# First stage of a two-layer backbone: token stores in pieces, third buffers, and scratch tiles that share room

## Chip, cores and metric

The kernel runs on one core of one Trainium2 chip. The metric is the device time of one execution in microseconds; before the change it is 5293.11 us, the median of three runs (5286.99 to 5300.15).

## What is computed

One inference step of a hybrid backbone with two layers. A layer normalises and modulates the tokens (256 context tokens and 2048 latent ones), projects them, runs four mixers on the projections, and maps their gated outputs back into the residual:

```python
h = (rms_norm(x) * (1.0 + scale) + shift).astype(dt)
(da_q, da_k, da_v, da_g, s5_u, s5_g, hg_q, hg_ff, hg_fb, hg_i, hg_g,
 mla_cq, mla_ckv, mla_kr, mla_g) = split_columns(h @ P["w_in"][l])
a_out, a_ctx = diff_attn_branch(...)
b_out, b_ctx = s5_branch(...)
c_out, c_ctx = hgrn_branch(...)
d_out, d_ctx = mla_branch(...)
mixed = jnp.concatenate([a_out, b_out, c_out, d_out], axis=-1)
x = (x.astype(F32) + gate * (mixed @ P["w_out"][l]).astype(F32)).astype(dt)
```

The change touches the projection of the keys, queries and values (`da_q`, `da_k`, `da_v`, part of the MLA inputs) and the tables that the state-space branch `s5_branch` needs: powers of the discretised diagonal transition matrix, its products with the input and output matrices, and the skip term `s5_d`.

## The kernel before

A layer has three parts: `first_stage`, `mixers`, `out_proj`. `first_stage` weaves two generators, `proj1` and `s5_build`; a scheduler decides with a simulated timeline in which order each engine gets their instructions, and each engine then runs its own list strictly in order. The order of PE in the mixers is written by hand. All stores and loads named below are issued by SP, one list too, so a store whose data are late holds up whatever stands behind it; only the value stores `VT` of the last block are issued by POOL.

**proj1** (L420) works on six blocks of 384 tokens. `h_block` (L275) normalises a block: PE transposes (`pst`, L299), ACT scales (`t32`, L304), DVE casts to the high part `hhi` (L171) and subtracts to the low part `hlo` (L173), for eight slices `kc` of 128 channels. `keep(i)` (L438) then stores both parts of the block to `HD` (L440), from where proj2 reads all tokens again. Five products `psF` follow (two of keys, two of queries, one of the MLA inputs; 24 matmuls each), each with `evac1` (L358): ACT copies (`x`), DVE rotates (`sh`, `rt`), ACT casts `sphi` and DVE subtracts `splo`, and three stores take them to `KD` or `QD` (L355). The MLA rows use the same tiles under the names `krhi` and `krlo`. Then come three value products `psT` (24 matmuls each); ACT copies each to `evT` (L499), which is stored to `VT` (L500). `sphi`, `splo` and `evT` have two buffers each.

**s5_build** (L1160) makes tables for 16 channel groups. `prep(gi)` runs on POOL (`wz`, `so`, with the one scratch tile `tw`) and DVE (`so` at L1286, `cp`, `brep`); `emit(gi)` has PE transpose `wz` (`pswz`, L1302) and multiply (`psk`, L1307), ACT copy both, and SP store `so` to `SC`. After every fourth `emit` DVE adds the skip term `Db` to four finished tables `mp` (L1311); the last such addition belongs to group 15. POOL then doubles a small table `b` four times (`double_table`, L1150) with the scratch tile `t3`, and from it makes eight pairs of tables `Eb`, 28 operations per pair, each stored by two `ED` stores (L1336). `Eb0`, `Eb1` and `Db` have room of their own, and `t3` is free once the discretisation is done, so the scheduler is free to put `Eb` work between the `prep` steps:

```python
    emit(15, *late)
    E.memset(b_[0][:, :, 0:1], 1.0)
    ...
    double_table(E, b_, ph, slice(0, 16), t3, 0, 4)
    ...
    for g0 in range(0, 16, 2):
        gs = slice(g0, g0 + 2)
        Eb = [pb.tile([128, 2, 257], F32, tag=f"Eb{i}", name=f"Eb{i}") for i in range(2)]
```

**mixers** begins with proj2 (L506), led by attention's first pass (`psS`, from `ks` and `qs`, which are loaded from `KD` and `QD`). proj2 loads the normalised tokens back (`h<-HD`, L521) and a weight block at a time (`w<-wF`, L532, one tile `w32`). ACT and DVE split the first two weight blocks into `whi` and `wlo`, POOL the later ones.

Of the kernel before, what the change touches and what calls it, by code (L numbers as in the profile page):

```python
# [10 lines left out]
F32 = mybir.dt.float32  # L11
F32R = mybir.dt.float32r
# [95 lines left out]

PR = (0, 0)
AVB = 2  # L110
PPB = 3
# [163 lines left out]
def h_block(g, l, tok0, n, p, hi, lo, mod):  # L275
    nc = g.nc
    xs, ds = [], []
    for t in range(n // 128):
        xt = p.tile([128, D], F32, tag="xt", name="xt", bufs=3)
        nc.sync.dma_start(xt, x_src(g, l, tok0 + t * 128))  # L280
        ss = p.tile([128, 1], F32, tag="ss", name="ss")
        junk = p.tile([128, D], BF16, tag="junk", name="junk", bufs=1)
        nc.scalar.activation(out=junk, in_=xt, func=AF.Square, accum_out=ss)
        r = p.tile([128, 1], F32, tag="r", name="r")
        rsqrt_col(g, p, r, ss, 1.0 / D, "rs")
        dg = p.tile([128, 128], F32, tag="dg", name="dg", bufs=4)
        nc.vector.tensor_scalar(dg, g.ident, r, None, ALU.mult)
        xs.append(xt)
        ds.append(dg)
    cut = min(max(LS - tok0, 0), n)  # L290
    if mod is not None:
        next(mod)
    for kc in range(8):
        if mod is not None and kc % 2 == 0:
            next(mod)
            next(mod)
        ps = pst(g, "mm", "pst")
        for t in range(n // 128):
            nc.tensor.matmul(ps[:, t * 128:(t + 1) * 128], lhsT=xs[t][:, kc * 128:(kc + 1) * 128], rhs=ds[t], start=True, stop=True)  # L299
        t32 = p.tile([128, 384], F32, tag="t32", name="t32")  # L300
        for a, b, gr in ((0, cut, 0), (cut, n, 1)):
            if b > a:
                sc, sh = g.scale[:, gr, kc:kc + 1], g.shift[:, gr, kc:kc + 1]
                nc.scalar.activation(out=t32[:, a:b], in_=ps[:, a:b], func=AF.Identity, bias=sh, scale=sc)  # L304
        split2(g, hi[:, kc, :], lo[:, kc, :], t32, "vec")
    if mod is not None:
        run(mod)
# [36 lines left out]
def store_kr(g, p, src, tok0, n):  # L344
    nc = g.nc
    hi = p.tile([128, 384], F32R, tag="sphi", name="krhi")[64:96, :n]
    lo = p.tile([128, 384], F32R, tag="splo", name="krlo")[64:96, :n]
    split2(g, hi, lo, src)
    nc.sync.dma_start(g.KRD[0, 0:32, tok0:tok0 + n], hi.bitcast(F32))
    nc.sync.dma_start(g.KRD[1, 0:32, tok0:tok0 + n], lo.bitcast(F32))  # L350
# [7 lines left out]
def evac1(g, l, p, kind, idx, ps, tok0, n):  # L358
    nc = g.nc
# [15 lines left out]
    r32 = rope(g, p, x32, (0, 128), tok0, n, "rp")  # L375
    hi = p.tile([128, 384], F32R, tag="sphi", name="sphi")
    lo = p.tile([128, 384], F32R, tag="splo", name="splo")
    split2(g, hi, lo, r32)
# [27 lines left out]
def cache_keys(g, l, p):  # L406
    nc = g.nc
    for i in range(2):
        kc32 = p.tile([128, 384], F32, tag="x32", name="kc32", bufs=1)
        nc.sync.dma_start(kc32[:, :256], g.A["cdk"][l, i])  # L410
        hi = p.tile([128, 384], F32R, tag="sphi", name="sphi")
        lo = p.tile([128, 384], F32R, tag="splo", name="splo")
        split2(g, hi[:, :256], lo[:, :256], kc32[:, :256])
        store_qk(g, g.KD, (0, 1, 0), i, hi[:, :256], lo[:, :256], slice(NT, NK))
# [5 lines left out]
def proj1(g, l):  # L420
    nc = g.nc
    N = 384
    with ExitStack() as es:
# [7 lines left out]
        def prep(i):  # L431
# [4 lines left out]
            hs[i] = (hi, lo)  # L436

        def keep(i):  # L438
            for part, x in enumerate(hs[i]):
                nc.sync.dma_start(g.HD[part, :, :, starts[i]:starts[i] + N], x.bitcast(F32))  # L440

# [24 lines left out]
        for kc in range(0, 8, 2):  # L466
            w32 = pws.tile([128, 2, 512], F32, tag="w32", name="wt32")
            nc.sync.dma_start(w32, g.A["wT"][l, :, kc:kc + 2, :])
            split2(g, wth[:, kc:kc + 2, :], wtl[:, kc:kc + 2, :], w32, "act", W1LO)
        keep(0)  # L470
        yield
        cache_keys(g, l, p)
        for i, tok0 in enumerate(starts):
            if 0 < i < len(starts) - 1:
                prep(i + 1)
                keep(i + 1)
            if i == 2 and l == 0:
# [4 lines left out]
            for k, (kind, idx, cols) in enumerate(FB1):  # L482
                if i == 0 and k == H1:
                    prep(1)
                    keep(1)
                m = len(cols)
# [5 lines left out]
            for t in range(N // 128):  # L492
# [3 lines left out]
                for kc in range(8):  # L496
                    mm3(nc, ps, hi[:, kc, ts_], lo[:, kc, ts_], wth[:, kc, :], wtl[:, kc, :], kc == 0, kc == 7)
                o = p.tile([128, 512], F32, tag="ev", name="evT")
                nc.scalar.copy(o, ps)  # L499
# [660 lines left out]
def s5_build(g, l, p1, pb):  # L1160
# [64 lines left out]
    yield 5  # L1225
    t3 = pb.tile([128, 16, 16], F32, name="t3")
    den, fr, fi, am1 = t16("den"), t16("fr"), t16("fi"), t16("am1")
# [26 lines left out]
    for i in range(2):  # L1254
# [7 lines left out]
        V.tensor_copy(pt[i][64:128, :, 0:8][:, :, ::-1], pv[64:128, :, 0:8])  # L1262
    Db = pb.tile([128, 16, 16], F32, name="Db")
    nc.sync.dma_start(Db.rearrange("p g h -> p (g h)"), g.A["s5_d"][l:l + 1, :].to_broadcast([128, 256]))
# [51 lines left out]
    for gi in range(16):  # L1316
# [4 lines left out]
        late = x  # L1321
    emit(15, *late)
    E.memset(b_[0][:, :, 0:1], 1.0)
    E.memset(b_[1][:, :, 0:1], 0.0)
    double_table(E, b_, ph, slice(0, 16), t3, 0, 4)
    yield 5
    for g0 in range(0, 16, 2):
        gs = slice(g0, g0 + 2)
        Eb = [pb.tile([128, 2, 257], F32, tag=f"Eb{i}", name=f"Eb{i}") for i in range(2)]
        te = t3.rearrange("p (a b) c -> p a (b c)", a=2)  # L1330
# [477 lines left out]
```

## Time and profile before

| | |
|---|---|
| median of three runs | 5293.11 us (5286.99 to 5300.15) |
| the profiled execution's own time | 5296.69 us |
| its span, first to last instruction | 5294.9 us |
| mean granted clock of TensorE | 0.935 |
| busy: PE, DVE, ACT, POOL | 89%, 72%, 60%, 21% |
| chain that ended last | PE 49%, DVE 18%, DMA 13%, ACT 10%, issue 4%, POOL 4% |
| DMA bytes | 599.37 MB |
| first stage, layer 0 | until the first weight load of proj2 at 453.75 us |
| first stage, layer 1 | until the first weight load of proj2 at 3098.75 us |

The shares are means over stages with different limits. The first stage takes about 450 us of each layer; the times below are microseconds from the start of the span, layer 1 begins at some 2640 us. "Idle before" in a row names what the engine waited for; a wait for several things is put down to the one that came last.

### The profile page before, as it was taken

The numbers are of one execution on the slowest core, as the hardware profiler recorded it, in microseconds if no ns is written. First come the engines' busy times: TensorE is split into PE (matmuls) and PEld (weight loads), VectorE is DVE, ScalarE is ACT, GpSimd is POOL, SyncE is SP. The second block draws the span as 40 slices with busy tenths as digits, with TensorE's granted clock in tenths as the row PEclk, the third lists the DMA queues.
The fourth block names the chain that finished last, engine by engine and source line by source line (L and its number), as shares of the span: only waits on it lengthen the run. The fifth ranks groups of instructions, "written<-read, shape, count | busy, mean of one in ns | idle before, by whom it ended". The sixth has DMA issues, their size and how long they took to land.

```text
span 5294.9 us, 81097 instructions
## 1 busy us (share of the span) xinstructions
PE 4724.9 (89%) x27920; PEld 3434.4 (65%) x27920; DVE 3835.7 (72%) x7616; ACT 3183.3 (60%) x7516; POOL 1089.4 (21%) x1323
## 2 busy tenths in 40 slices
PE   6787999999998997898987879999999989989899
PEld 5676767677665664445776757676776656654477
DVE  7655767676668886896676657676766688879877
ACT  3225878777777783235433258787777777743354
POOL 4651222222210000000227712222222100000022
PEclk8998999999998997899999989999999989989999
DMA  6555233433332124415445452334333321241253
GB/s 219 170 174 154 87 105 96 130 116 104 92 88 75 47 57 129 130 50 148 157 155 200 159 167 86 108 94 130 116 103 93 88 73 48 54 117 52 75 155 126
DMA packets 507523, 599.37 MB, mean 113 GB/s; under 512 B 147630, under 2 KB 414806, under 8 KB 507110
## 3 DMA queue, kind: packets, MB, share of 16 engines
q1 hardware_dynamic: 506630, 592.61, 37.3%
q8 instruction: 220, 3.60, 0.3%
q14 instruction: 193, 1.58, 0.1%
q0 software_dynamic: 480, 1.57, 0.1%
HBM read 378.42 MB, written 215.18 MB: 112 GB/s over the span
## 4 chain that ended last, share of the span: by engine, by line
PE 49%; DVE 18%; DMA 13%; ACT 10%; issue 4%; POOL 4%; SPq 1%; ACTq 0%; DVEq 0%; POOLq 0%
PE psav L858 5%; PE psS L870 4%; PE psF L177 4%; PE psF L178 4%; PE psF L179 4%; PE psS L817 4%; PE psmav L950 3%; ACT junk L820 3%; PE psM L961 2%; DVE nm L818 2%; DVE a L872 2%; DVE mnm L927 2%; ACT pp L871 2%; PE psM L926 2%; PE pshg L1018 2%
## 5 line engine op out<-in xcount | busy, mean ns | idle before, releaser
L818 DVE TENSOR_REDUCE nm<-psS 128x1 f32<-128x512 f32 (+1 forms) x1312 | 790.5, 626 | 351.7 <-PE psS L817 340.5
L820 ACT ACTIVATE junk<-psS,nm 128x512 bf16<-128x512 f32 (+1 forms) x1312 | 848.7, 647 | 202.2 <-DVE nm L818 182.4
L871 ACT ACTIVATE pp<-psS 128x512 f32<-128x512 f32 (+1 forms) x1184 | 654.5, 594 | 165.7 <-PE psS L870 159.6
L177 PE MATMUL psF<-h,whi 128*128 128x288 f32 x2304 | 697.9, 303 | 32.8 <-ACT whi L169 32.8
L872 DVE SCALAR_TENSOR_TENSOR a<-pp,nlam 128x512 f32<-128x512 f32 (+1 forms) x592 | 510.3, 864 | 257.6 <-ACT pp L871 256.9
L178 PE MATMUL psF<-h,whi 128*128 128x288 f32 x2304 | 687.9, 299 | 0.0
L179 PE MATMUL psF<-h,wlo 128*128 128x288 f32 x2304 | 685.1, 297 | 1.8 <-DVE wlo L173 1.8
L964 ACT ACTIVATE me<-psM 128x512 f32<-128x512 f32 (+1 forms) x592 | 345.6, 590 | 440.8 <-PE psM L963 395.1
L817 PE MATMUL psS<-ks,qs 96*128 96x512 f32 (+1 forms) x1312 | 544.5, 425 | 58.9 <-ACT junk L820 37.7
L870 PE MATMUL psS<-qs,ks 98*128 98x512 f32 (+1 forms) x1184 | 440.6, 436 | 53.9 <-ACT junk L820 38.7
L177 PEld LDWEIGHTS psF<-h,whi 128*128 128x128 f32 x2304 | 444.7, 193 | 65.3 <-ACT whi L169 34.5
L171 POOL CAST whi<-w 128x1024 fp32r<-128x1024 f32 x140 | 153.2, 1094 | 1622.0 <-PE psF L178 1299.7
L178 PEld LDWEIGHTS psF<-h,whi 128*128 128x128 f32 x2304 | 444.8, 193 | 54.8
L927 DVE TENSOR_REDUCE mnm<-psM 128x1 f32<-128x512 f32 (+1 forms) x656 | 394.1, 623 | 70.9 <-PE psM L926 69.0
L179 PEld LDWEIGHTS psF<-h,wlo 128*128 128x128 f32 x2304 | 441.5, 192 | 3.1 <-DVE wlo L173 3.1
L817 PEld LDWEIGHTS psS<-ks,qs 96*128 96x128 f32 x1312 | 255.2, 197 | 165.5 <-ACT junk L820 98.4
L870 PEld LDWEIGHTS psS<-qs,ks 98*128 98x128 f32 x1184 | 203.3, 192 | 236.3 <-ACT junk L820 136.4
L173 POOL TENSOR_TENSOR wlo<-w,whi 128x1024 fp32r<-128x1024 f32 x140 | 350.3, 2502 | 11.2
L967 DVE TENSOR_TENSOR macc<-macc,me 128x1024 f32<-128x1024 f32 x256 | 311.2, 1216 | 45.0 <-ACT me L964 44.2
L950 PE MATMUL psmav<-me,mv 128*64 128x512 f32 (+1 forms) x1184 | 318.0, 631 | 13.7 <-ACT me L964 7.9
L858 PE MATMUL psav<-a,dav 128*64 128x512 f32 (+1 forms) x1184 | 309.5, 643 | 18.2 <-DVE a L872 18.2
L961 PE MATMUL psM<-qs,ks 98*128 98x512 f32 (+1 forms) x592 | 269.8, 456 | 49.2 <-ACT me L964 21.6
(451 smaller groups left out, 10191.2 us busy)
## 6 DMA issues: line engine op xcount, KB each, us to landing
w<-wF SPq DMA_DIRECT2D x152, 512.0 KB
h<-HD SPq DMA_DIRECT2D x64, 576.0 KB
wmod<-w_mod SPq DMA_DIRECT2D x48, 512.0 KB
HD<-hhi SPq DMA_DIRECT2D x12, 1536.0 KB
HD<-hlo SPq DMA_DIRECT2D x12, 1536.0 KB
GX<-ev SPq DMA_DIRECT2D x128, 144.0 KB
gt<-GX SPq DMA_DIRECT2D x36, 512.0 KB
PF<-ev SPq DMA_DIRECT2D x96, 144.0 KB
```

The costliest lines, as they stand in the source:

```text
L177: nc.tensor.matmul(out, lhsT=w_hi, rhs=x_hi, start=start, stop=False)
L178: nc.tensor.matmul(out, lhsT=w_hi, rhs=x_lo, start=False, stop=False)
L179: nc.tensor.matmul(out, lhsT=w_lo, rhs=x_hi, start=False, stop=stop)
L817: nc.tensor.matmul(ps[:, :kn], lhsT=qs[0:96, i, t * 128:(t + 1) * 128], rhs=key_cols(ks[i], k0, kn)[0:96], start=True, stop=True)
L818: nc.vector.tensor_reduce(nm[:, i, t, ci:ci + 1], ps[:, :kn], axis=AX.X, op=ALU.max, negate=True)
L820: nc.scalar.activation(out=junk[:, :kn], in_=ps[:, :kn], func=AF.Exp, bias=nm[:, i, t, ci:ci + 1], accum_out=sm[:, i, t, ci:ci + 1])
L858: x = nc.tensor.matmul(av[hh * 64:(hh + 1) * 64, :n], lhsT=v[:, kt, hh * 64:(hh + 1) * 64], rhs=aa[:, hh, :n], start=(ki == 0), stop=(ki = ...
L870: nc.tensor.matmul(ps[:, :n], lhsT=key_cols(ks[2 * hh + m], kt * 128, 128), rhs=qs[:, 2 * hh + m, :n], start=True, stop=True)
L871: nc.scalar.activation(out=pp[:, m, :n], in_=ps[:, :n], func=AF.Exp)
L872: last = nc.vector.scalar_tensor_tensor(aa[:, hh, :n], pp[:, 1, :n], nlam, pp[:, 0, :n], ALU.mult, ALU.add)
L927: nc.vector.tensor_reduce(nm[:, i, t, ci:ci + 1], ps[:, :kn], axis=AX.X, op=ALU.max, negate=True)
L950: x = nc.tensor.matmul(av[i * 64:(i + 1) * 64, :n], lhsT=v[:, kts[ki], i * 64:(i + 1) * 64], rhs=e[:, i, :n], start=(ki == 0), stop=(ki == ...
```

## The change

Three things are done. The two stores of a whole block (1536 KB each) become eight stores of 384 KB, issued inside `h_block` after every second slice. `sphi`/`krhi`, `splo`/`krlo` and `evT` get a third buffer. The room for it comes from the state-space scratch: `t3` and `Db` share one buffer, so `t3` is made a second time once `Db` has been used for the last time, and the `Eb` tiles take the two buffers of `so`.

```diff
+HDP = 2
...
         split2(g, hi[:, kc, :], lo[:, kc, :], t32, "vec")
+        if kc % HDP == HDP - 1:
+            k0 = kc + 1 - HDP
+            for part, x in enumerate((hi, lo)):
+                nc.sync.dma_start(g.HD[part, :, k0:kc + 1, tok0:tok0 + n], x[:, k0:kc + 1, :].bitcast(F32))
...
-    hi = p.tile([128, 384], F32R, tag="sphi", name="krhi")[64:96, :n]
-    lo = p.tile([128, 384], F32R, tag="splo", name="krlo")[64:96, :n]
+    hi = p.tile([128, 384], F32R, tag="sphi", name="krhi", bufs=3)[64:96, :n]
+    lo = p.tile([128, 384], F32R, tag="splo", name="krlo", bufs=3)[64:96, :n]
...
-    hi = p.tile([128, 384], F32R, tag="sphi", name="sphi")
-    lo = p.tile([128, 384], F32R, tag="splo", name="splo")
+    hi = p.tile([128, 384], F32R, tag="sphi", name="sphi", bufs=3)
+    lo = p.tile([128, 384], F32R, tag="splo", name="splo", bufs=3)
...
-        def keep(i):
-            for part, x in enumerate(hs[i]):
-                nc.sync.dma_start(g.HD[part, :, :, starts[i]:starts[i] + N], x.bitcast(F32))
...
-        keep(0)
...
-                keep(i + 1)
...
-                    keep(1)
...
-                o = p.tile([128, 512], F32, tag="ev", name="evT")
+                o = p.tile([128, 512], F32, tag="ev", name="evT", bufs=3)
...
-    t3 = pb.tile([128, 16, 16], F32, name="t3")
+    t3 = pb.tile([128, 16, 16], F32, tag="t3", name="t3")
...
-    Db = pb.tile([128, 16, 16], F32, name="Db")
+    Db = pb.tile([128, 16, 16], F32, tag="t3", name="Db")
...
     emit(15, *late)
+    t3 = pb.tile([128, 16, 16], F32, tag="t3", name="t3")
     E.memset(b_[0][:, :, 0:1], 1.0)
...
-        Eb = [pb.tile([128, 2, 257], F32, tag=f"Eb{i}", name=f"Eb{i}") for i in range(2)]
+        Eb = [p1.tile([128, 2, 257], F32, tag="so", name=f"Eb{i}") for i in range(2)]
```

The scheduler orders both programs anew. On POOL, in layer 0, the first `Eb` pair stands between the `prep` operations (`wz`, `so`, `tw`) of the third and fourth channel group before the change (`t` is the scratch `t3`, numbers tell buffers apart):

```order
L252 TENSOR_TENSOR Eb_2626<-Eb_2626,ph_544 128x2x128
L255 TENSOR_TENSOR Eb_2627<-Eb_2626,ph_545 128x2x128
L253 TENSOR_TENSOR tw<-pws_946,bb_938 128x128
L257 TENSOR_TENSOR Eb_2627<-Eb_2627,t_911 128x2x64
L254 TENSOR_TENSOR wz_1258<-wz_1258,tw 128x8x16
L253 TENSOR_TENSOR t_911<-Eb_2627,ph_545 128x256
L1281 TENSOR_TENSOR so<-pq_947,c_931 128x128
```

After it, the last `prep` ends before the b table begins, with one small copy of `Eb` between:

```order
L1280 TENSOR_TENSOR tw<-pq_954,c_938 128x128
L1281 TENSOR_TENSOR so<-so,tw 128x128
L1283 TENSOR_TENSOR tw<-pq_954,c_937 128x128
L1334 COPY Eb_2651<-ph_552 128x2
L254 TENSOR_TENSOR t_2584<-b_936,ph_537 128x16
L255 TENSOR_TENSOR b_935<-b_935,t_2584 128x16
L257 TENSOR_TENSOR t_2584<-b_936,ph_536 128x16
```

All 16 `prep` steps now stand ahead of the b table, and all eight `Eb` pairs behind it, one after the other.

On SP, in layer 0, the last `ED` stores stood among the stores of block 4 before (`KD`, `QD`, `HD`), with the first loads of `h` close behind them:

```order
L1336 DMA ED<-Eb_3199 128x514
L355 DMA KD<-sphi 4x32x384
L1336 DMA ED<-Eb_3200 128x514
L355 DMA KD<-splo 4x32x384
L440 DMA HD<-hhi 1024x1x384
L440 DMA HD<-hlo 1024x1x384
L355 DMA KD<-sphi 4x32x384
L521 DMA h_4145<-HD 128x4x288 x2
```

After, the last `ED` pair stands at the end of the first loads of the mixers:

```order
L803 DMA qs<-QD 96x4x512
L320 DMA cos<-rcos 128x288
L321 DMA sin<-rsin 128x288
L803 DMA qs_7953<-QD 96x4x256
L1335 DMA ED<-Eb_3230 128x514
L1335 DMA ED<-Eb_3231 128x514
L530 DMA w_4336<-wF 128x1024
L519 DMA h_4182<-HD 128x4x288 x2
L519 DMA h_4185<-HD 128x4x288 x2
L530 DMA w_4342<-wF 128x1024
```

The first `w` load and the loads of `h` for the first half now stand behind the eighth pair, and the loads `dav`, `qs`, `cos`, `sin`, which stood between the first and the second `w` load, stand ahead of both. Of the other pairs, pair 1 and 2 stand among the `KD` and `QD` stores of block 4, 3 and 4 among and behind its `VT` stores, 5 in the `QD` stores of block 5, 6 ahead of the first `qs` and `ks` loads, 7 among the small weight loads. In layer 1 the order is alike.

## Rows read from the trace of the kernel before

**Rows 1.** View by stretches (start:end, us, busy us of PE, PEld, DVE, ACT, POOL, clock, DMA, GB/s).

```profile
110.00:335.00 225.00, 182.67 (x897) 159.49 (x896) 146.61 (x320) 59.69 (x133) 168.82 (x366) 0.91 0.49 160
```

**Rows 2.** Waits of ACT, 60 to 460 us: us in total, times, longest.

```profile
ACT sphi L169 <- DMA KD<-sphi: 45.1, 6, 12.3
```

**Rows 3.** Waits of DVE, 60 to 460 us.

```profile
DVE krlo L173 <- DMA QD<-splo: 25.7, 6, 8.2
```

**Rows 4.** Waits of DVE in layer 1, 2700 to 3120 us.

```profile
DVE krlo L173 <- DMA QD<-splo: 15.5, 4, 8.0
```

**Rows 5.** Chain of waits, 2640 to 3200 us: start, us, what.

```profile
2862.01 5.17 DMA ED<-Eb
...
2896.18 8.84 DMA ED<-Eb
...
2928.01 6.54 DMA ED<-Eb
...
2952.39 7.96 DMA ED<-Eb
...
3001.19 15.72 DMA KD<-sphi
...
3039.62 2.39 DMA ED<-Eb
```

**Rows 6.** Timeline of SP's queue, layer 1: start, us, engine, line, operation.

```profile
2997.02 0.57 SPq L440 DMA_DIRECT2D HD<-hhi  x1
...
3004.55 2.87 SPq L1336 DMA_DIRECT2D ED<-Eb  x1
...
3013.82 1.67 SPq L1336 DMA_DIRECT2D ED<-Eb  x1
```

**Rows 7.** Timeline of DVE, the last Db addition of each layer.

```profile
343.15 0.22 DVE L1311 TENSOR_TENSOR mp<-mp,Db 128x64 f32<-128x64 f32 x1
...
3029.10 0.31 DVE L1311 TENSOR_TENSOR mp<-mp,Db 128x64 f32<-128x64 f32 x1
```

**Rows 8.** Timeline of POOL, layer 0, ends of the last two Eb groups.

```profile
340.08 0.72 POOL L257 TENSOR_TENSOR Eb<-Eb,t 128x256 f32<-128x256 f32 x1
343.66 0.21 POOL L1332 COPY Eb<-b 128x32 f32<-128x32 f32 x1 [2.86 <-DMA ED<-Eb]
...
355.71 0.92 POOL L257 TENSOR_TENSOR Eb<-Eb,t 128x256 f32<-128x256 f32 x1
```

**Rows 9.** Timeline of SP's queue, first weight loads of proj2.

```profile
453.75 0.71 SPq L532 DMA_DIRECT2D w<-wF  x1
...
469.13 0.42 SPq L532 DMA_DIRECT2D w<-wF  x1
...
3098.75 0.95 SPq L532 DMA_DIRECT2D w<-wF  x1
...
3114.28 13.88 SPq L532 DMA_DIRECT2D w<-wF  x2
```

**Rows 10.** Line L1307 in layer 0: ns min/median/max, first and last start.

```profile
L1307 PE MATMUL psk<-cp,brep x64: 363/366/766, 116.7 to 341.6; 128*128 128x240 f32 x64
```

**Rows 11.** Line L1307 in layer 1.

```profile
L1307 PE MATMUL psk<-cp,brep x64: 363/368/768, 2805.4 to 3022.1; 128*128 128x240 f32 x64
```

**Rows 12.** Timeline of POOL, layer 1, ends of the last two Eb groups.

```profile
3004.24 0.73 POOL L257 TENSOR_TENSOR Eb<-Eb,t 128x256 f32<-128x256 f32 x1
...
3017.66 0.53 POOL L1332 COPY Eb<-b 128x32 f32<-128x32 f32 x1 [5.42 <-DMA ED<-Eb]
...
3034.16 0.73 POOL L257 TENSOR_TENSOR Eb<-Eb,t 128x256 f32<-128x256 f32 x1
```

**Rows 13.** Timeline of PE, first products of proj2.

```profile
465.81 0.61 PE L179 MATMUL psF<-h,wlo 128*128 128x288 f32 x1 [0.47 <-DVE wlo L173]
...
480.77 0.61 PE L177 MATMUL psF<-h,whi 128*128 128x288 f32 x1 [8.55 <-ACT whi L169]
...
3126.60 0.61 PE L177 MATMUL psF<-h,whi 128*128 128x288 f32 x1 [9.20 <-ACT whi L169]
```

More of the change, by code (lines that the diff above doesn't have):

```diff
@@ L410, in cache_keys @@
         nc.sync.dma_start(kc32[:, :256], g.A["cdk"][l, i])
-        hi = p.tile([128, 384], F32R, tag="sphi", name="sphi")
-        lo = p.tile([128, 384], F32R, tag="splo", name="splo")
+        hi = p.tile([128, 384], F32R, tag="sphi", name="sphi", bufs=3)
+        lo = p.tile([128, 384], F32R, tag="splo", name="splo", bufs=3)
         split2(g, hi[:, :256], lo[:, :256], kc32[:, :256])
```

## The prediction

> **What bounds the kernel now.** I read the busy times by stretch first, then the waits of DVE and ACT, then the timelines of POOL and SP, and last the chain of waits. In each layer the kernel runs a first stage (token products `psF` and `psT` woven with the state-space tables) and then the mixers, whose first weight load `w<-wF` starts proj2. From there on PE is the busiest engine, so what moves the end is when proj2's first products start. From 110 to 335 us, the table work of layer 0, PE is busy 182.67 of 225 us [rows 1]; the other 42 us are stalls. The third-buffer parts of the change aim at two rows: ACT idles 45.1 us because `sphi` still waits for its own store to KD [rows 2], and DVE idles 25.7 us, six times, because `krlo` waits for a QD store [rows 3], 15.5 us in layer 1 [rows 4]. The store in pieces aims at a third: in layer 1 a KD store takes 15.72 us on the chain [rows 5], and 4 us ahead of it SP had issued the first of two 1.5 MB HD stores [rows 6].
>
> **What moves.** The room sharing is the large part, and it moves work that these rows do not name. Before, POOL fills its gaps between the 16 `prep` steps with the eight `Eb` groups (28 operations each), so that seven of the eight are done when the last Db addition runs at 343.15 [rows 7, 8]. After, `t3` lies in Db's place and the `Eb` tiles in those of `so`: the b table can't start before that addition, and no `Eb` group before all `so` tiles are stored. POOL then runs b table and eight groups in one tail, each group waiting until the two ED stores of the one before have landed. And SP's order has ED pair 8 directly ahead of the first `w<-wF`, so proj2 starts behind that tail. Before, SP reached that load with all ED stores long issued, at 453.75 and 3098.75 [rows 9].
>
> **When the tail starts.** PE's instruction order has the last table product `psk` behind 717 token products of layer 0 where 781 stood ahead of it, and in layer 1 behind 786 where there were 929. At the pace between first and last `psk`, (341.6 − 116.7) / (781 − 124) = 0.342 us a product [rows 10], 64 fewer are 21.9 us; in layer 1 (3022.1 − 2805.4) / (929 − 284) = 0.336 us [rows 11] times 143 is 48.0 us. The third buffers give back DVE's `krlo` waits; four of six blocks lie ahead of the tail, so 25.7 × 4/6 = 17.1 us in layer 0, 10.3 us in layer 1. PE has other stalls, so I take half: 8.6 and 5.2 us (bounds: nothing, if other waits fill in, and all of PE's 42 us [rows 1]). The Db addition then falls at 343.15 − 21.9 − 8.6 = 312.6 and at 3029.10 − 48.0 − 5.2 = 2975.9 [rows 7].
>
> **How long the tail is.** The b table is a group's loop of four doublings at half its widths; a group takes 343.66 to 356.63 = 13.0 us [rows 8], and I take 10 us (an estimate from that, bounds half of it and all of it). For a group with its wait for the stores the trace has two samples of consecutive ends: in layer 0 from 340.80 to 356.63, 15.8 us, of which 2.86 us is the wait [rows 8]; in layer 1 from 4.97 to 34.89 past 3000, 29.9 us, where SP issued the first ED store at 3004.55 and the second, behind QD stores, only at 3013.82, so that POOL idled 5.42 us for the first alone [rows 6, 12] and ran a few prep operations between. The ED stores on the chain of layer 1 take 5.17, 8.84, 6.54, 7.96 and 2.39 us [rows 5], 6.2 us in the mean, which would make 13.0 + 6.2 = 19.2 us a group. I take 17.5, midway between the quiet sample and that mean, nearer the quiet end than the 29.9 because most pairs of the tail are issued after the last HD store. Eight groups: 140 us.
>
> **The sum.** Layer 0: 312.6 + 10 + 140 = 462.6 for the first `w`, against 453.75. The second `w` uses the same tile and cannot be issued until the first is split, 12.1 us on (453.75 to 465.81 [rows 9, 13]): 474.7, against 469.13, where before other loads held it. From there to its products is 11.6 us (469.13 to 480.77): 486.3 against 480.77, **5.5 us later**. Layer 1: 2975.9 + 150 = 3125.9; + 12.1 = 3138.0; + 12.3 (3114.28 to 3126.60 [rows 9, 13]) = 3150.3 against 3126.60, **23.7 us later**. Together + 29.2 us. The four `h<-HD` loads of the first half, which before stood in SP's order far ahead, among the last block's stores, now follow the first `w`; I cost them at nothing, since the load and split of that `w` (12.1 us) cover them; without that cover they would cost some microseconds a layer.
>
> **Parts that cost nothing by themselves.** The pieces make 96 HD stores where there were 24, 36 more a layer. At 0.57 us each on SP [rows 6] that is 20 us of SP time, spread over some 250 us in which SP mostly waits for data; uncovered it is up to + 20 us a layer, if SP becomes late for KD and QD stores. At the start, eight pieces stand between the weight loads of layer 0 where two stores stood behind them: 0 to 5 us (8 × 0.57), taken as 0. The third `evT` removes a wait of ACT that lies beside PE's work; PE's gain from it is in the half taken above. The two 1.5 MB stores and the eight of 384 KB write the same bytes. The Trainium skill, "DMA: Bandwidth & Descriptors", section "Bandwidth", speaks against the pieces: transfers should be at least 1 MiB for three quarters of the peak, with 0.95 us for 64 KB and 6.15 us for 1 MB. Between these, by an estimate on that page's figures, four 384 KB stores take about 1.8 us longer than one of 1.5 MB, some 22 us of transfer time a layer (12 such stores); if all of it lay on the path, the sum would be near + 73 us. The trace speaks for less: the 16 DMA engines are busy only 0.49 of the time in this stretch [rows 1], so the sum goes without it.
>
> The profiled execution took 5296.69 us, the median of the runs is 3.6 us lower (5293.11). So 5296.69 + 29.2 − 3.6 = **5322 us**, 0.55% slower. What a measurement of this kernel can tell from no change is about 0.3%, 16 us.
>
> **Rivals.**
> - *The quiet tail (no change).* ED stores land as in layer 0's sample, 15.8 us a group [rows 8]. That takes 8 × 1.7 = 13.6 us from each layer: − 8.1 and + 10.1, + 2 us, 5295. For it: after its first pairs no HD store runs beside the tail, and KD bursts behind smaller HD stores should be shorter. Against it: KD, QD, VT stores and `ks` loads run beside it, and its only sample has light traffic.
> - *The stage itself gets faster (faster).* The place is the way to the Db addition: POOL's preps no longer stand between `Eb` operations, and ACT and DVE lose their store waits, so PE's 42 us of stalls [rows 1] shrink by half, 21 us instead of 8.6, and in layer 1 by about as much. With the quiet pace: 2 − 12 − 14 = − 24 us, 5269; with nearly all stalls gone some 5245. It decides from the point at which, at 15.8 us a group, the Db addition comes before about 303 and 2967 us. For it: rows 2 and 3. Against it: DVE is as busy as before and its order has nearly the same work ahead of the last `so`.
> - *SP and POOL hold each other (much slower).* As in layer 1's sample [rows 6, 12], ED stores stand behind KD, QD and VT stores whose data are late, and those behind ED stores whose groups are late. At 20 us a group: + 20 us a layer, 5362; at half-and-half of the two samples, 22.9: + 43 a layer, 5409. It decides where a group takes over 19 us.
> - *The change does not do what it says.* The pieces wait in SP's queue so that KD and QD stores land no earlier and the third buffers fill up: the 8.6 and 5.2 us are not given back, 5336.
>
> **Chances.** Forecast 0.40, heavy coupling 0.13, no relief 0.05, together 0.58 slower; quiet tail 0.24, no change; faster stage 0.18. The first is the largest because the tail of 150 us is given by the program, and only its start and its pace are estimates. The range 5270 to 5366 reaches from the faster case (half of it lies below) to the coupled one at 20 us a group. The likeliest case's own range is 5306 to 5338 (16.5 to 18.5 us a group).
>
> **What would show it.** Right: on POOL's timeline `Eb` operations only after the last Db addition, at about 313 and 2976 us, eight groups at 17 to 18 us ending in ED stores at about 463 and 3126, `w<-wF` right behind, PE idle for `whi` longer than before in layer 1, and a wait of POOL `Eb` on the ED stores of 30 us or more a layer; `sphi` waiting for KD on ACT much less than 45 us. Wrong: the first `w` at or before 453 and 3099 us (pace or start mis-sized), the second `w` held by another load, or a mixer stage that absorbs a late start.

## The result and the profile after

The changed kernel takes 5355.96 us (median of six runs, 5334.39 to 5364.40), the kernel before in the same comparison 5294.59 us. The ratio is 1.0111 [1.0099, 1.0124]: slower by 61 us, about twice the forecast 0.55%. The profiled execution took 5361.38 us, with a span of 5359.6 us against 5294.9; the times below are from these two spans.

Where the 64.7 us of span lie can be read at three marks that both traces have: the first `nmx` of DVE in each layer (attention has its first row of scores), and the first `xt` load of layer 1.

| mark | before | after | lost since the mark before |
|---|---|---|---|
| attention's first row, layer 0 | 521.79 | 523.88 | +2.1 |
| layer 1 begins | 2680.99 | 2685.17 | +2.1 |
| attention's first row, layer 1 | 3167.58 | 3213.78 | +42.0 |
| end of the span | 5294.9 | 5359.6 | +18.5 |

So layer 0 costs 4.2 us, the first stage of layer 1 42.0, and the mixers of layer 1, which the change does not touch, 18.5.

**Layer 0.** DVE's timeline has the last Db addition at 306.12, where 343.15 stood in [rows 7]:

```profile
306.12 0.22 DVE L1309 TENSOR_TENSOR mp<-mp,Db 128x64 f32<-128x64 f32 x1
```

POOL's timeline behind it: the b table waits for this addition, and the first `Eb` group starts 6.8 us after the b table does. The last line is from the second group, which waits little for ED.

```profile
306.42 0.23 POOL L254 TENSOR_TENSOR t<-b,ph 128x16 f32<-128x16 f32 x1 [1.08 <-DVE mp L1309]
...
313.24 0.21 POOL L1331 COPY Eb<-b 128x32 f32<-128x32 f32 x1
...
332.98 0.62 POOL L1331 COPY Eb<-b 128x32 f32<-128x32 f32 x1 [0.93 <-DMA ED<-Eb]
```

The last ED pair is issued at 460.00, and SP's timeline shows what stands behind it (answering to [rows 9]; start, us, engine, line, operation):

```profile
460.00 0.90 SPq L1335 DMA_DIRECT2D ED<-Eb  x2
462.00 0.33 SPq L530 DMA_DIRECT2D w<-wF  x1
469.88 2.38 SPq L519 DMA_DIRECT2D h<-HD  x4
473.43 10.09 SPq L530 DMA_DIRECT2D w<-wF  x2
```

The `h<-HD` loads stand directly behind the first `w`, but are issued 7.9 us after it; by the experiments below they wait until the last ED pair has landed. PE's timeline, answering to [rows 13]; its 25.22 us of idle time are put down to the `h` loads, which came last:

```profile
474.08 0.58 PE L178 MATMUL psF<-h,whi 128*128 128x288 f32 x1 [25.22 <-DMA h<-HD]
477.31 0.61 PE L179 MATMUL psF<-h,whi 128*128 128x288 f32 x1 [2.65 <-DMA h<-HD]
```

**Layer 1.** DVE's timeline, the last Db addition (3029.10 before):

```profile
2999.93 0.23 DVE L1309 TENSOR_TENSOR mp<-mp,Db 128x64 f32<-128x64 f32 x1 [0.17 <-ACT mp L1306]
```

SP's timeline. The first line holds the last ED stores, four in 16.40 us:

```profile
3140.12 16.40 SPq L1335 DMA_DIRECT2D ED<-Eb  x4
3156.58 0.42 SPq L530 DMA_DIRECT2D w<-wF  x1
3159.05 2.71 SPq L519 DMA_DIRECT2D h<-HD  x4
3162.80 0.35 SPq L530 DMA_DIRECT2D w<-wF  x1
```

PE's waits, 2690 to 3200 us; before, its longest row there was 17.5 us for `whi`, and it waited for no `h`:

```profile
PE psF L178 <- DMA h<-HD: 38.9, 1, 38.9
PE psS L815 <- DMA ks<-KD: 18.7, 1, 18.7
```

By stretches (columns as in [rows 1]), the 60 us ahead of these products: PE is busy 18.38 us of them.

```profile
3104.00:3164.00 60.00, 18.38 (x25) 7.21 (x25) 18.31 (x29) 19.92 (x50) 26.17 (x70) 0.50 0.80 225
```

**The waits that the change aimed at.** In layer 0 ACT's `sphi` waits 4.8 us for KD instead of 45.1 [rows 2], and DVE's `krlo` waits for ACT alone instead of 25.7 us for QD [rows 3]. In layer 1 another wait has grown. ACT's waits, 2690 to 3150 us, after:

```profile
ACT junk L284 <- DMA xt<-X: 59.4, 9, 17.5
ACT sphi L170 <- DVE rt L333: 44.2, 17, 7.4
...
ACT krhi L170 <- DMA KD<-sphi: 12.8, 2, 8.2
```

The same view before (`junk` is the first operation on a block's tokens `xt`):

```profile
ACT sphi L169 <- DMA KD<-sphi: 25.2, 4, 9.5
...
ACT junk L283 <- DMA xt<-X: 20.6, 9, 6.9
ACT evT L499 <- DMA VT<-evT: 19.6, 3, 11.6
```

Four of these loads are among the longest pieces of the chain of waits after, 2660 to 3220 us, of which `xt` loads hold 7.8%; before, 2660 to 3180 us, they hold 2.7%, in pieces of up to 7.96 us:

```profile
2767.88 11.73 DMA xt<-X
...
2816.84 12.13 DMA xt<-X
...
2890.25 10.15 DMA xt<-X
...
2949.56 9.46 DMA xt<-X
```

SP's timeline ahead of the second of them: pieces (L310) and KD stores (L360) take turns, and the `xt` pair follows.

```profile
2811.22 1.50 SPq L360 DMA_DIRECT2D KD<-sphi  x1
...
2812.82 1.16 SPq L310 DMA_DIRECT2D HD<-hlo  x1
2814.04 1.14 SPq L360 DMA_DIRECT2D KD<-sphi  x1
2815.27 1.47 SPq L360 DMA_DIRECT2D KD<-splo  x1
2816.84 4.28 SPq L281 DMA_DIRECT2D xt<-X  x2
```

### The profile page after: what moved, and what is told of

Read it like the earlier page. It is cut to its first block, busy times and chain, and to the rows that moved or that the text cites. A ratio compares the mean times of both kernels' runs of the same rounds, so it can differ in the third digit from the quotient of the medians.

```text
span 5359.6 us, 81266 instructions
## 1 busy us (share of the span) xinstructions
PE 4729.3 (88%) x27920; PEld 3453.4 (64%) x27920; DVE 3805.9 (71%) x7616; ACT 3178.5 (59%) x7516; POOL 1077.9 (20%) x1323
## 4 chain that ended last, share of the span: by engine, by line
PE 51%; DVE 18%; DMA 12%; ACT 10%; issue 5%; POOL 3%; SPq 1%; ACTq 0%; DVEq 0%; POOLq 0%
PE psav L856 5%; PE psF L178 4%; PE psF L179 4%; PE psS L868 4%; PE psF L180 4%; PE psS L815 4%; PE psmav L948 3%; ACT junk L818 3%; PE psM L959 2%; DVE nm L816 2%; DVE a L870 2%; ACT pp L869 2%; PE psM L961 2%; PE psM L960 2%; PE psM L924 2%
## 5 line engine op out<-in xcount | busy, mean ns | idle before, releaser
L174 POOL TENSOR_TENSOR wlo<-w,whi 128x1024 fp32r<-128x1024 f32 x140 | 349.9, 2499 | 11.2
L948 PE MATMUL psmav<-me,mv 128*64 128x512 f32 (+1 forms) x1184 | 306.3, 619 | 13.6 <-ACT me L962 8.7
L924 PE MATMUL psM<-ks,qs 96*128 96x512 f32 (+1 forms) x656 | 259.9, 435 | 56.5 <-DMA ks<-KRD 23.5
```

The lines of the kernel that those rows point to most:

```text
L948: x = nc.tensor.matmul(av[i * 64:(i + 1) * 64, :n], lhsT=v[:, kts[ki], i * 64:(i + 1) * 64], rhs=e[:, i, :n], start=(ki == 0), stop=(ki == ...
```

## The experiments

The leading theory was that the room sharing makes the loss (a serial tail of b table and `Eb` groups, and at its end proj2's `h`), and that pieces and third buffers matter little. Rivals were the pieces (more DMA instructions on SP), the third buffers, and the order of ED stores on SP. The table has the median and the ratio to the kernel before, measured beside it, and, from each profiled execution, the difference to the span of before, split at the marks above. A profiled execution can lie up to 25 us off its kernel's median, so single stages are read to about that.

| run | median us | ratio | layer 0 to first row | mixers 0 | first stage 1 | mixers 1 |
|---|---|---|---|---|---|---|
| the change | 5355.96 | 1.0111 [1.0099, 1.0124] | +2 | +2 | +42 | +19 |
| share | 5353.78 | 1.0098 [1.0078, 1.0119] | +24 | +2 | +34 | −2 |
| share_eb | 5334.30 | 1.0071 [1.0042, 1.0100] | +20 | 0 | +26 | −14 |
| nopieces | 5357.04 | 1.0112 [1.0097, 1.0127] | +24 | +7 | +28 | +5 |
| pieces | 5286.04 | 0.9976 [0.9964, 0.9987] | −27 | −4 | +14 | −2 |
| third_buf | 5334.03 | 1.0064 [1.0047, 1.0080] | +3 | −1 | +8 | +32 |
| evt_room | 5316.92 | 1.0036 [1.0021, 1.0052] | −1 | −12 | +9 | +18 |
| pieces_third | 5295.20 | 0.9995 [0.9979, 1.0011] | −25 | −1 | +24 | +3 |
| ed_pool_queue | 5304.75 | 1.0016 [1.0002, 1.0029] | −5 | −17 | +33 | −8 |
| change_h_elsewhere | 5338.88 | 1.0073 [1.0048, 1.0097] | −18 | +2 | +39 | +11 |
| halves | 5270.09 | 0.9952 [0.9936, 0.9969] | −33 | −2 | +14 | −4 |
| halves_first_layer | 5288.65 | 0.9971 [0.9954, 0.9988] | −31 | −7 | −8 | +12 |
| halves_h_elsewhere | 5301.43 | 0.9999 [0.9986, 1.0012] | −24 | +1 | +13 | +15 |

### The room sharing alone (share), and half of it (share_eb)

```diff
-    t3 = pb.tile([128, 16, 16], F32, name="t3")
+    t3 = pb.tile([128, 16, 16], F32, tag="t3", name="t3")
...
-    Db = pb.tile([128, 16, 16], F32, name="Db")
+    Db = pb.tile([128, 16, 16], F32, tag="t3", name="Db")
...
     emit(15, *late)
+    t3 = pb.tile([128, 16, 16], F32, tag="t3", name="t3")
...
-        Eb = [pb.tile([128, 2, 257], F32, tag=f"Eb{i}", name=f"Eb{i}") for i in range(2)]
+        Eb = [p1.tile([128, 2, 257], F32, tag="so", name=f"Eb{i}") for i in range(2)]
```

share_eb has the last pair of lines only.

> Room sharing alone (t3 with Db, Eb in so), whole-block HD stores, two buffers. If the tail is what costs: POOL's eight Eb groups again in one run behind the last Db addition, at 18 to 19 us a group, first w of proj2 right behind ED pair 8 in layer 1, 150 to 157 us behind the Db addition (layer 1: Db addition at about 2976, first w at about 3130, products 25 to 30 us later than before); 20 to 40 us slower than before in all. If the pieces or the third buffers are what costs: within 10 us of before.

> Only the Eb tiles in the buffers of so; t3 and Db keep their own room, so the b table is made early. If the tail of Eb groups behind the last so is what costs: slower than before by 25 to 50 us, the b table's 10 us a layer less than sharing both. If it is the wait of the b table for Db: within 10 us of before.

The sharing alone gives a loss as large as the change's: 1.0098 (56 us, more than the 20 to 40 expected), the change 1.0111. The places differ, though: share loses 24 us in layer 0 and 34 in layer 1's first stage, the change 2, 42, and 19 in layer 1's mixers. The Db addition of layer 0 comes at 297.3, but the tail lasts 170.9 us (to `w` at 468.2) where the change has 155.9 (306.1 to 462.0). POOL's waits in share, 60 to 500 us, against 38.2 us for the same row in the change:

```profile
POOL Eb L1333 <- DMA ED<-Eb: 46.8, 12, 11.6
```

PE's timeline in share, the first product of proj2:

```profile
494.56 0.58 PE L177 MATMUL psF<-h,whi 128*128 128x288 f32 x1 [25.10 <-DMA h<-HD]
```

The `Eb` part by itself gives the tail too: in share_eb the Db addition comes at 294.9 and `w` at 465.0. What `t3` adds to it is within what single runs tell.

### The pieces alone, and the change without them (pieces, nopieces)

```diff
+HDP = 2
...
+        if kc % HDP == HDP - 1:
+            k0 = kc + 1 - HDP
+            for part, x in enumerate((hi, lo)):
+                nc.sync.dma_start(g.HD[part, :, k0:kc + 1, tok0:tok0 + n], x[:, k0:kc + 1, :].bitcast(F32))
...
-        keep(0)
```

`keep` and its other calls go too; nopieces is the change without these lines.

> HD stores in four pieces alone, everything else as before. If the pieces cost by themselves (they stand in SP's queue ahead of the xt loads of the next block): ACT's wait for xt in layer 1 grows from about 25 to about 59 us as in the changed kernel, first psk of layer 1 some 20 us later, proj2 of layer 1 10 to 30 us later, 10 to 30 us slower in all. If the tail alone costs: within 10 us of before, as no Eb group stands behind the Db addition of group 15 but the last one or two.

> The change without the pieces: room sharing and third buffers, two whole-block HD stores. Its order has the last psk of layer 0 behind 626 token products (717 in the change), of layer 1 behind 768 (786). If the pieces make the tail of layer 1 start late: Db addition of layer 1 back at about 2976 (2999.9 in the change), first w at about 3132 (3156.6), 25 to 40 us faster than the change, 20 to 35 us slower than before. If they don't matter: Db addition within 8 us of 2999.9 and the time within 15 us of the change's 5356.

By themselves the pieces make the kernel faster, 0.9976, by the first stage of layer 0 (−27). There ACT's wait of 45.1 us [rows 2] falls to 13.9 without any third buffer. Yet taking them out of the change gains nothing (1.0112 against 1.0111): two effects cancel. nopieces has the longer tails, 178.2 us in layer 0 (294.3 to 472.5) and 162.4 in layer 1 (3008.8 to 3171.2; the change 156.7). But in layer 1 its Db addition comes 296.1 us after the layer's start (2712.6), share's 298.6, and the change's 314.8.

That the pieces make layer 1 late does not take the sharing. By DVE's timelines the last Db addition of layer 1, counted from the layer's start, falls into four groups that do not overlap: 341.5 to 349.9 us in the five traces with neither (before, evt_room, third_buf, halves_first_layer, base_fixed_order), 358.8 to 372.2 in the four with pieces or halves and no sharing (pieces, pieces_third, halves, halves_h_elsewhere), 296.1 to 298.6 in the three with sharing and no pieces (share, share_eb, nopieces), and 308.6 to 314.8 in the four with both (the change, ed_pool_queue, change_h_elsewhere, change_fixed_order). The first stage of layer 1 says the same: +14 for pieces against 0 before, +42 for the change against +28 for nopieces. The delay does not grow with the number of stores: 12 more a layer (halves, 369.3) delay the addition at least as much as 36 more (pieces, 364.1).

Under which name ACT waits depends on the buffers. With two of `sphi` the wait for KD doubles in layer 1, where it fell in layer 0: 25.2 us before, and in pieces (2660 to 3120 us)

```profile
ACT sphi L170 <- DMA KD<-sphi: 51.3, 7, 10.0
```

With three the wait for the next block's tokens grows, without any sharing too; pieces_third, 2665 to 3125 us:

```profile
ACT junk L284 <- DMA xt<-X: 47.0, 8, 13.1
```

From 2690 to 3150 us it is 59.4, 51.1 and 51.9 us in the change, ed_pool_queue and change_h_elsewhere, which have pieces and third buffers, but 29.5 in share, 36.0 in nopieces and 26.8 in pieces, which lack one or both. Why the pieces gain in layer 0 and cost in layer 1, no run shows.

### The third buffers alone (third_buf, evt_room, pieces_third)

The third buffers need room, which was taken by moving `evT` into the tiles of the first stage's weights, a change of its own. evt_room is this move alone, third_buf both, pieces_third both with the pieces.

```diff
-                o = p.tile([128, 512], F32, tag="ev", name="evT")
+                o = pws.tile([128, 512], F32, tag="w32", name="evT")
...
-    hi = p.tile([128, 384], F32R, tag="sphi", name="sphi")
-    lo = p.tile([128, 384], F32R, tag="splo", name="splo")
+    hi = p.tile([128, 384], F32R, tag="sphi", name="sphi", bufs=3)
+    lo = p.tile([128, 384], F32R, tag="splo", name="splo", bufs=3)
```

> Third buffers for sphi and splo alone, without the tail: their room comes from the two evT tiles, which take the buffers of the weight tiles w32 once the weights are split (evT stays at two). If the store waits of ACT and DVE were worth what I took (8.6 and 5.2 us): 5 to 20 us faster than before, the wait of sphi for KD under 15 us in layer 0. If the stage is held by other things: within 5 us of before although those waits are gone.

> Control for the third buffers: before with the two evT tiles in the buffers of the weight tiles w32, sphi and splo with two buffers as before. If the third buffers are worth something by themselves: slower than third_buf, whose first products of proj2 stand at +3 and +7 us against before, so +10 us or more here. If they are worth nothing: +0 to +10 us at the same two places. What the mixers do (+33 us in layer 1 of third_buf) is either the same here (then it comes from the evT room) or not (then from the order that the scheduler happened to find).

> Pieces together with third sphi and splo buffers (room from evT in the w32 buffers), no tail. If the two help each other, as the change assumes: proj2 of layer 0 starts 30 us or more ahead of before, and the time is 10 us or more under the 5286 of the pieces alone. If the store waits are already gone with the pieces, or the evT tiles in the weight buffers are what costs: 5285 to 5335.

ACT's waits in evt_room, 60 to 460 us:

```profile
ACT sphi L169 <- DMA KD<-sphi: 47.2, 7, 14.2
...
ACT evT L499 <- DMA VT<-evT: 29.6, 4, 10.1
ACT sphi L169 <- DVE rt L328: 29.0, 15, 4.2
...
ACT krhi L169 <- DMA QD<-sphi: 20.6, 5, 7.5
```

The same view in third_buf; the `sphi` row is gone, and the time stands under other names:

```profile
ACT evT L499 <- DMA VT<-evT: 47.9, 4, 26.4
ACT sphi L169 <- DVE rt L328: 46.3, 22, 4.1
...
ACT krhi L169 <- DMA KD<-sphi: 20.2, 3, 8.5
```

The waits for `evT` and for DVE's `rt` have grown by 18.3 and 17.3 us; `krhi` waits for a store as long as in evt_room, only for another one. The first stages differ by +3 and +8 in third_buf and by −1 and +9 in evt_room: the third `sphi` and `splo` removed the 45 us row and gained nothing there. The medians are 17 us apart, against third_buf, and the traces put the difference into the mixers (−1 and +32, −12 and +18); why is not shown. Beside the pieces the third buffers cost (0.9995 against 0.9976), with `evT`'s move in it. A third `evT` in room of its own was not tried.

### The ED stores from POOL's queue (ed_pool_queue)

```diff
-            nc.sync.dma_start(g.ED[i, :, gs], Eb[i])
+            nc.gpsimd.dma_start(g.ED[i, :, gs], Eb[i])
```

> The change with the 16 ED stores of a layer issued by POOL's queue instead of SP's; room and buffers as in the change. If SP and POOL hold each other (ED stores wait behind KD and QD stores, and these behind ED stores): a group takes 15 to 17 us instead of 18.5, the last blocks of the first stage end earlier, the first products of proj2 come 15 to 30 us earlier in each layer, 30 to 55 us faster than the change. If only the tail's own length and the room that proj2's h tiles take over from Eb count: still a wait of PE for h<-HD after the last ED store, 10 to 25 us faster than the change, slower than before.

This takes back most of the loss (1.0016), but not through the tail: from the Db addition to the `h` loads it lasts 158.1 us in layer 0 (304.9 to 462.95) and 155.5 in layer 1 (2968.0 to 3123.5), where the change has 163.8 and 159.1. Of the 62 us of span between it and the change, 7 and 9 lie in the first stages and 46 in the two layers' mixers, which hold no ED store; why those are faster is not shown. What the run does tell is in SP's timeline, layer 0. The first `w` now goes out early, and the `h` loads of the first half, next in the list, are issued 22.8 us later:

```profile
440.13 0.48 SPq L530 DMA_DIRECT2D w<-wF  x1
462.95 2.27 SPq L519 DMA_DIRECT2D h<-HD  x4
```

PE's timeline:

```profile
467.05 0.58 PE L178 MATMUL psF<-h,whi 128*128 128x288 f32 x1 [38.91 <-DMA h<-HD]
```

`whi` is ready at 448.26 there, so PE waits for `h` alone, and no place in SP's list explains why: nothing stands ahead of it. What is left is room. The pool of this `h` (`p2a`) lies where `so` lay, and with the sharing the `Eb` tiles are there until their last stores have landed. The last ED store is issued 2.6 us ahead of the loads, on POOL's timeline,

```profile
460.32 0.56 POOL L1335 DMA_DIRECT2D ED<-Eb  x1 [0.30 <-POOL Eb L258]
```

and 2.7 us ahead of them in layer 1 (3120.82 and 3123.50).

### proj2's tiles elsewhere (change_h_elsewhere)

```diff
-        pa = es.enter_context(pool(g, "p2a", 1, "right"))
+        pa = es.enter_context(pool(g, "p2a", 1))
```

The pools `p2`, `p2h` and `mu` move to the other side of the memory in the same way; all else in the program is as in the change. The scheduler then also puts the first loads of `h` and `w` ahead of ED pairs 7 and 8, so room and order change together here; room alone is what ed_pool_queue tells.

> The change, with the four pools of proj2 on the other side of SBUF, so that its h and w tiles take over the room of proj1's tiles and not that of so and Eb. The first stage's order is the change's, unaltered up to ED pair 6; the first h and w loads now wait for PE's last psT and stand ahead of ED pairs 7 and 8. If the room is the gate (h<-HD waits until ED pair 8 has landed): PE's wait for h<-HD of 25 and 39 us falls under 10 us, the first products of proj2 come 25 to 35 us earlier in layer 0 (474 in the change) and 30 to 45 us earlier in layer 1 (3163.6), 45 to 75 us faster than the change. If POOL's tail or SP's queue is the gate: products within 10 us of the change's, since tail, queue and stores are as they were; under 20 us faster.

That bears out the room. In layer 0 the first half's `h` loads go out ahead of the last ED pair, PE waits 0.8 us for `h` instead of 27.9, and its first product comes 20.8 us earlier, at 453.25 instead of 474.08 (PE's timeline):

```profile
453.25 0.44 PE L178 MATMUL psF<-h,whi 128*128 128x288 f32 x1
```

In layer 1 the first product comes at 3113.94 instead of 3163.57 (19.4 us of this because the layer starts earlier), but the second half's `h` loads stand in SP's list behind the last ED stores. SP's timeline:

```profile
3131.52 13.04 SPq L1335 DMA_DIRECT2D ED<-Eb  x3
...
3147.91 2.48 SPq L519 DMA_DIRECT2D h<-HD  x4
```

PE's timeline:

```profile
3152.42 0.58 PE L178 MATMUL psF<-h,whi 128*128 128x288 f32 x1 [25.01 <-DMA h<-HD]
```

So the gate of room, once open, is replaced by the gate of order, and most of layer 1's loss stays (+39). The ratio falls from 1.0111 to 1.0073, 17 us by medians, where 45 to 75 were expected if the room were the gate.

### The pieces in halves (halves, halves_first_layer, halves_h_elsewhere)

`HDP = 4` in the pieces' edit makes four stores of 768 KB out of the two of 1536 KB; nothing else is changed. halves_first_layer has them in layer 0 alone, halves_h_elsewhere adds the move of proj2's pools.

```diff
+HDP = 4
...
-        if kc % HDP == HDP - 1:
+        if l == 0 and kc % HDP == HDP - 1:
```

> HD stores in two halves per part (768 KB, after every fourth slice) instead of four pieces, nothing else changed against before. If what the pieces give is that stores of a block do not come in one burst, half of it: 5 to 9 us faster than before. If any earlier start does: as the pieces, 10 to 14 us.

> Halves in layer 0 and whole-block stores in layer 1. In halves, proj2 of layer 0 starts 33 us earlier than before and the first stage of layer 1 gives some 15 us back. If smaller stores harm in layer 1 by themselves (more SP issues beside out_proj's loads and stores): those 15 us stay, 5255 to 5265. If layer 1's order is only another draw: 5265 to 5290.

> Halves, with proj2's pools on the other side as in change_h_elsewhere. Without the tail the room is not the gate, so nothing is to be gained there: within 10 us of halves (5270); slower if the first h loads, which halves issues among block 4's stores, now wait for proj1's end: products of proj2 5 to 15 us later in each layer.

halves is the fastest kernel of the study, 5270.09 us, 0.9952 [0.9936, 0.9969]. The gain is in layer 0, on the chain of waits from 20 to 460 us, by line. Before:

```profile
by line: DMA QD<-sphi 9.5%; DMA KD<-sphi 8.3%; DMA QD<-splo 5.9%; DMA VT<-evT 5.9%; DMA ks<-KD 4.2%; DMA SC<-so 4.0%; issue 3.0%; DMA kc<-cdk 2.4%; SPq L355 1.9%; SPq L1313 1.9%; DMA h<-HD 1.8%; DVE splo L173 1.7%; DVE hlo L173 1.6%; POOL E
```

halves:

```profile
by line: DMA SC<-so 5.7%; DMA xt<-x_s 3.8%; DMA ks<-KD 2.7%; issue 2.6%; DMA w<-wF 2.6%; PE psF L180 2.2%; DMA QD<-splo 2.2%; DMA ED<-Eb 2.2%; PE psF L178 2.1%; PE psF L179 2.1%; DMA h<-HD 1.8%; PE psT L179 1.8%; PE psT L180 1.8%; PE psT L1
```

The stores of `sphi` that held 17.8% of it are gone from the first places. In layer 1 halves start the tail of the stage later, as the pieces do (the last Db addition 369.3 us after the layer's start, 341.5 in halves_first_layer; first stage +14 against −8). But by medians halves_first_layer is no faster than halves, and its trace is its fastest execution, 25 us under its median; so what whole-block stores in layer 1 would gain in all stays open. Moving proj2's pools takes the gain away again (0.9999): in layer 0 attention's first row comes 8.6 us later than in halves, within the 5 to 15 us expected if the first `h` loads must wait for proj1's end, and the mixers of layer 1 take 19 us more (+15 against −4), which no wait named here explains; a new order of the whole program comes with each such edit.

### Both kernels with PE's order fixed (base_fixed_order, change_fixed_order)

```diff
-MAN = False
+MAN = True
```

PE's order in the later part of the mixers is then the program's own in both kernels, instead of the scheduler's. This tells apart two theories of the 18.5 us that the untouched mixers of layer 1 lose: another order that the scheduler happened to make, or a late start that collides with something.

> Before, with the order of PE in the second part of the mixers (attention beside the state-space branches) given by the program and not by the scheduler. First stages as before within 3 us. The mixers take whatever this order takes, between 30 us less and 100 us more than before; it is the base for change_fixed_order.

> The change, with the same order of PE in the mixers as base_fixed_order. If the scheduler's draw of the mixers' order made the 18 us in layer 1: 40 to 50 us slower than base_fixed_order, of which 3 and 43 us in the two first stages and under 6 us in the mixers of both layers together. If the late start or colliding transfers made them: 60 to 70 us slower than base_fixed_order, 15 to 20 us of it again in the mixers of layer 1.

The two take 5617.48 and 5658.68 us (ratios 1.0598 and 1.0685 to the kernel before), 41.2 us apart by medians and 40.2 by spans (5623.0 and 5663.2). Between them, the first stage and mixers of layer 0 differ by −0.5 and −5.4, layer 1's first stage by +39.5, its mixers by +6.5. So layer 1's first stage loses what it lost in the change itself (+42.0), with the same wait of PE, 3200 to 3600 us, in change_fixed_order:

```profile
PE psF L178 <- DMA h<-HD: 39.9, 1, 39.9
PE psS L815 <- DMA ks<-KD: 18.2, 1, 18.2
```

The mixers lose a third of the 18.5. That fits a redrawn order and not a cost of starting late; since these kernels are 6% slower than the others, it is support and not proof. The table speaks for it too: in the kernels above, the untouched mixers of layer 1 come out between −14 and +32 us.

## Why the prediction was right and wrong

The direction and the mechanism hold: the room sharing turns `Eb` into a tail behind the last Db addition, proj2 starts behind it, and share alone loses as much. The size was missed: two terms of the sum were put at nothing, the pieces' price in layer 1 (16 to 19 of the 19.8 us by which its tail starts late) and the mixers (18.5 us in layer 1). By the prediction's steps, at the marks above, 64.7 us are the forecast 29.2, less 1.3 in layer 0, plus 18.3 in layer 1's first stage, plus 18.5 in its mixers.

- **When the tail starts, layer 0.** Forecast 312.6, measured 306.1, but not by the term that was to give it. PE's line of the table products, after, 60 to 460 us:

```profile
L1305 PE MATMUL psk<-cp,brep x64: 363/367/770, 131.1 to 303.9; 128*128 128x240 f32 x64
```

  The count of 717 products holds, but 211 of them (139 `psF`, 72 `psT`), not 124, stand ahead of the first `psk`. Behind it the pace is (303.9 − 131.1) / (717 − 211) = 0.342 us a product, the same as before, so the third buffers gave nothing back there. What came early is the stretch ahead of the first `psk`: 87 more products took 14.4 us more. Share and share_eb, without third buffers, have the addition at 297.3 and 294.9.
- **How long it is.** The b table took 6.8 us, not 10. A group took (460.00 − 330.33) / 7 = 18.5 us, from the first ED pair's issue to the last's, not 17.5. To `w` it is 155.9 us instead of 150. The two misses of layer 0 cancel, by luck: `w` at 462.00, forecast 462.6.
- **`h<-HD` costed at nothing: right within 2 us, for a reason that was incomplete.** The step took the loads' place in SP's list as their only condition. They have a second, the room that the last `Eb` tiles hold, and the two come at nearly the same time: in layer 0 `whi` is ready at 472.14 (ACT's cast from 471.10, 1.04 us) and the first product runs at 474.08; in layer 1 at 3161.50 and 3163.57. So the 25.2 and 38.9 us of PE under the name of `h` are the end of the tail, which the forecast had through `w`. The second condition matters for any repair: taking ED off SP opens the first gate and not the second, moving the tiles the other way round.
- **When the tail starts, layer 1: the largest miss of the sum.** Forecast 2975.9, measured 2999.9; 4.2 of the 24.0 is layer 0's, 19.8 is this layer's. The step that failed is the pieces at nothing: 36 more stores a layer were to cost nothing, and up to +20 us a layer uncovered, if SP became late. Without pieces the addition stands 296.1 and 298.6 us after the layer's start (nopieces, share), where the forecast had 294.9 (2975.9 − 2680.99); with them 314.8. Some 6 us of that gap may be order alone, since nopieces and share have 768 and 770 products ahead of the last `psk` and the change 786, at 0.36 us each. But the pieces alone, without sharing, make the addition 16 us later too (364.1, 348.1 before). That the bound of 20 us was about met is no support for its reason, 0.57 us of SP for each store, since halves, with a third of the additional stores, delay it as much. In the change it was `xt` that came late, rather than KD and QD: four such loads took 9.5 to 12.1 us from issue to landing; how much of the delay is SP's order, the transfers themselves or the scheduler's new order is not separated. The 5.2 us to be given back by `krlo` were not seen.
- **The tail in layer 1** took 156.7 us, 6.7 over forecast. From `w` to attention's first row it then made up 11.6 us (57.2 us, 68.8 before), where the forecast had 3.5 (27.2 us late at `w`, 23.7 at the products): the second `w` followed 6.2 us after the first, not 12.1. Together 19.8 + 6.7 − 8.1 is the 18.3 above, but for rounding.
- **The mixers costed at nothing.** True of layer 0 (+2.1), and not of layer 1. The forecast had no term for a scheduler that orders the untouched part anew.
- **The third buffers.** Their rows went as forecast, but nothing came back: third_buf and evt_room differ by 4 us or less in the first stages. The waits moved to `evT` and to DVE's `rt`.
- **The pieces as a loss by their size.** The Trainium skill, "DMA: Bandwidth & Descriptors", section "Bandwidth", asks for transfers of 1 MiB or more; its times are of loads issued from GpSimd, and these are stores from SP's queue. The runs go against it as a guide here: 768 KB and 384 KB stores give 0.9952 and 0.9976 of the time with 1536 KB. In layer 1 the pieces do cost (+14 us of its first stage), but a price for each additional transfer, as in the prediction's estimate from that page (22 us a layer), does not fit: halves cost as much there with a third of the additional stores, and in layer 0 both gain.
- **The rivals.** The quiet tail did not come (18.5 us a group). The faster stage got two thirds of the way to its 303 us in layer 0 (312.6 forecast, 306.1 measured) and nowhere in layer 1. SP and POOL hold each other as in the third rival only without the pieces: less the b table's 6.8 us, layer 0's tail is 20.5 us a group in share and 21.4 in nopieces; with the pieces the pace stays under the 19 us from which it would decide.

What stays open is by what path the pieces cost layer 1's first stage some 14 us while they gain in layer 0, and what makes single mixers faster or slower.

## What to carry to other kernels

Sharing scratch room gives an order to work that had none: what was free to fill gaps becomes a tail, and whatever is allocated over that room next, here the loads of the following stage, waits for the tail's last store. Ask of each freed buffer who lies there next, and of each store who stands behind it in its queue. A total can hide what a part does: the parts nearly add up here (pieces −0.24%, third `sphi` and `splo` +0.28% over their control, sharing +0.98%, all three +1.11%), but the pieces' small gain is 27 us won in one layer and 14 lost in the other. With a scheduler that orders anew, some 20 us of a difference may come from parts that no edit touched, so look at marks along the run, not at the total alone.

## What was not expected of the hardware

- Stores of half and a quarter of the size did not slow this kernel as a whole. In layer 0 `sphi` waits 13.9 us for KD with 384 KB pieces and 45.1 us with 1536 KB stores, although the DMA engines are no less busy, 0.53 of the time against 0.49 [rows 1] (pieces, 110 to 335 us, by stretches):

```profile
110.00:335.00 225.00, 184.36 (x954) 161.09 (x953) 150.47 (x330) 67.03 (x152) 186.57 (x419) 0.95 0.53 175
```

  In layer 1 the same wait doubles with the pieces (51.3 against 25.2 us). So the size of a store does not by itself decide the wait of the stores behind it.

- In the stall of layer 1, 3104 to 3164 us, with PE busy 18.38 of 60 us, the granted clock is 0.50, the 1.2 GHz level, while the DMA engines are busy 0.80 of the time: PE ran at 0.92 in the table stretch of layer 0 (110 to 335 us), with 188.69 of 225 us busy. In layer 1 POOL's longest wait of `Eb` for an ED store is 16.1 us, in layer 0 it is 8.1 us.
